# The fourth token form laid with the other three, and one weight unit of each feed-forward group laid at places of its own

## The chip, the core and the metric

The kernel runs on one NeuronCore of a Trainium2 chip. TensorE (PE in the profile) multiplies; before each matmul the stationary operand is loaded into the array by a weight load of its own (PEld). VectorE (DVE), ScalarE (ACT) and GpSimd (POOL) do the element-wise work, SyncE (SP) issues most transfers. The metric is the device time of one execution in microseconds, the median of several runs.

## The reference

A decoder trunk of two layers over 512 tokens of width 1024. Each layer has two feed-forward blocks (inner width 2816), a token mixer (latent attention in layer 0, a sparse attention with compressed, selected and window branches in layer 1) with four memory heads beside it, and three layer norms.

```python
def swiglu(x, w_gu, w_down):
    g, u = jnp.split(x @ w_gu, 2, axis=-1)
    return (jax.nn.silu(g) * u) @ w_down

for layer in range(DEPTH):
    x = layer_norm(DN_ALPHA * x + 0.5 * swiglu(x, ffn_w_gu[layer, 0], ffn_w_down[layer, 0]), ...)
    ...
    x = layer_norm(DN_ALPHA * x + mix, ln_g[layer, 1], ln_b[layer, 1])
    x = layer_norm(DN_ALPHA * x + 0.5 * swiglu(x, ffn_w_gu[layer, 1], ffn_w_down[layer, 1]), ...)
    if layer == N_A_LAYERS - 1:
        shared = nsa_shared_kv(x, nsa_w_kv, cmp_pos, cmp_w1, cmp_b1, cmp_w2)
```

The element type is float32.

## The kernel before

Every float32 operand of a product is held as two parts: `hi`, the value rounded by a cast on ACT, and `lo`, the remainder, taken by DVE (`split`, L199 and L200). A product is then three matmuls, hi by hi, hi by lo and lo by hi. Weights come in units of 128 x 1024 (`wraw`, four places), and each unit is split into `whi` and `wlo`. `prep` does this for the unit that is next in the list of `_unit_order`; `ring` gives it its two places, of seven that are used in turn (three in `wring`, four in `W.extra`).

A feed-forward block (`ffn`) works in five groups of four or five inner slices of 128 (`GROUPS`, 22 slices in all). In a group the slices are computed first, then `by_units` (or `token_major` in the last group) multiplies them by the group's down weights, with 512 columns for a matmul (L411 to L416).

A slice marked `d` is computed by `seven` as seven quarter products in place of eight, in the manner of Strassen: the tokens are 1024 x 512, seen as four quarters, and besides two of the quarters themselves (`quarters`, views of `xhi` and `xlo`) four sums and differences of quarters are used, the token forms `F.t[1]` to `F.t[4]`, made once for each block by `token_forms`. A quarter product (`quarter`, L376, L377 and L380) is twelve matmuls of 256 columns; the weight is the stationary operand, the token quarter streams past it. The weight units of such a slice are `g0` (two quarters on `xhi`/`xlo`), `g1` (form 4, then form 1), `g2` (forms 2 and 3) and `g3` (one quarter, half a unit). A slice marked `s` is computed in the plain way by `feature_major` (L363, L365, L368), 24 matmuls for each half of the tokens and each of its two weights (gate and up). In the first group of a block with `halves` (all blocks but the first of layer 1) the six units of the three `s` slices are held together and go through the first half of the tokens, then through the second.

The order of work on each engine is set by the framework from the program's own order and from when it reckons that operands and places are free; a change of places can thus move instructions.

Where things lie in a partition of SBUF, in bytes from its start, as the program is built: the places of all weight units are at multiples of 256; `xhi`, `xlo` and the forms 1 to 3 are at 192 past a multiple of 256 (`F.xp` begins with an offset of 448 bytes); form 4 is at a multiple of 256, since `open_f` puts an offset of 320 bytes ahead of it. A step of 128 columns is 512 bytes, so an operand keeps this remainder from matmul to matmul. `hhi` and `hlo`, the slices' results and the stationary operand of the down product, are at multiples of 256.

`norm_tile` writes the squares that it needs only as a sum into a scratch tile `junk` (L323, L324), which has a place of its own in the pool `F.sm`.

```python
        for i in (1, 2, 3, 0, 4):
            for e in "hl":
                if i:
                    F.fm.tile([P, 4, 256], F32, tag=f"t{i}{e}", name="place")
            if not i:
                F.fm.tile([P, 80], F32, name="offset")
```

## Time and profile before

| | us |
|---|---|
| median of 3 runs | 1853.71 (1851.89 to 1856.44) |
| the profiled execution | 1853.84 |
| its span, first to last instruction | 1852.1 |
| PE busy | 1830.8 |
| PE weight loads busy | 1650.6 |
| DVE busy | 1463.3 |
| ACT busy | 869.8 |
| POOL busy | 162.6 |

What lies around the span is 1.7 us. TensorE's granted clock is 0.999 over the span, so it ran at the higher of its two levels (2.4 GHz) throughout. Matmuls overlap: the duration of one runs past the start of the next, so what a matmul costs in a stream is read from start to start and not from its duration. A stretch of matmuls without a wait is priced by the start of its first, the start of the first that follows it, and the count between.

### The profile page before, as it was taken

Reading aid. Unit: us, or ns where it says so; the run is one execution under the profiler, and the core shown is the slowest. Engines: PE = TensorE matmul, PEld = TensorE weight load, DVE = VectorE, ACT = ScalarE, POOL = GpSimd, SP = SyncE. Lnnn points to the kernel's source line nnn. Section 1 sums busy time; section 2 is a strip of 40 time slices with the busy share of each in tenths; the row PEclk is TensorE's granted clock in tenths of the full one; section 3 lists DMA queues with packets and bytes.
Section 4 is the critical chain, followed back from the end, with each engine's and each line's share of the span. In section 5 each row is a group of like instructions: output and inputs, shape, how many; then the busy total and the mean of one; then the engine's idle time right before and its main releaser. Section 6 shows DMA issues by size and latency. Waiting matters only on the chain.

```text
span 1852.1 us, 31917 instructions
## 1 busy us (share of the span) xinstructions
PE 1830.8 (99%) x12772; PEld 1650.6 (89%) x12772; DVE 1463.3 (79%) x2365; ACT 869.8 (47%) x1439; POOL 162.6 (9%) x185
## 2 busy tenths in 40 slices
PE   9999999999999999999999999999999999999998
PEld 8899899896789899999999998998956789999997
DVE  8788789758668789788897987987567478887887
ACT  6344345456555335334653433444466444434432
POOL 0000000025500000000100000001255200000000
PEclk9999999999999999999999999999999999999999
DMA  7333335531134233234433323334321323323322
GB/s 243 117 110 118 111 106 154 178 103 34 59 114 149 80 103 126 81 108 143 132 123 109 126 87 108 114 121 158 109 47 28 114 76 130 114 80 115 118 80 77
DMA packets 60277, 203.86 MB, mean 110 GB/s; under 512 B 7008, under 2 KB 7792, under 8 KB 60128
## 3 DMA queue, kind: packets, MB, share of 16 engines
q1 hardware_dynamic: 57424, 194.44, 32.5%
q0 software_dynamic: 2416, 7.11, 1.3%
q8 instruction: 101, 1.65, 0.4%
q14 instruction: 48, 0.39, 0.1%
q10 hardware_dynamic: 288, 0.26, 0.0%
HBM read 188.16 MB, written 7.34 MB: 106 GB/s over the span
## 4 chain that ended last, share of the span: by engine, by line
PE 91%; DVE 4%; ACT 2%; DMA 1%; issue 1%; POOL 1%; POOLq 0%; SPq 0%; DVEq 0%; ACTq 0%
PE bank L376 13%; PE bank L380 13%; PE bank L377 13%; PE bank L411 4%; PE bank L412 4%; PE bank L413 4%; PE bank L415 4%; PE bank L414 4%; PE bank L416 4%; PE bank L365 3%; PE bank L368 3%; PE bank L363 3%; PE tb L671 2%; PE o L699 2%; PE s L1243 1%; PE bank L352 1%
## 5 line engine op out<-in xcount | busy, mean ns | idle before, releaser
L199 ACT CAST whi<-wraw 128x1024 fp32r<-128x1024 f32 (+2 forms) x475 | 460.1, 978 | 550.7 <-PE bank L416 243.9
L200 DVE TENSOR_TENSOR wlo<-wraw,whi 128x1024 fp32r<-128x1024 f32 (+2 forms) x475 | 535.1, 1132 | 131.3 <-ACT whi L199 130.4
L376 PE MATMUL bank<-t,whi 128*128 128x256 f32 x1232 | 298.4, 278 | 0.0
L377 PE MATMUL bank<-t,whi 128*128 128x256 f32 x1232 | 297.9, 278 | 0.0
L377 PEld LDWEIGHTS bank<-t,whi 128*128 128x128 f32 x1232 | 231.9, 188 | 0.0
L376 PEld LDWEIGHTS bank<-t,whi 128*128 128x128 f32 x1232 | 231.9, 188 | 0.0
L376 PE MATMUL bank<-xhi,whi 128*128 128x256 f32 x924 | 222.0, 277 | 0.0
L377 PE MATMUL bank<-xlo,whi 128*128 128x256 f32 x924 | 222.0, 277 | 0.0
L380 PE MATMUL bank<-t,wlo 128*128 128x256 f32 x1232 | 191.8, 278 | 0.0
L376 PEld LDWEIGHTS bank<-xhi,whi 128*128 128x128 f32 x924 | 173.6, 188 | 0.6
L377 PEld LDWEIGHTS bank<-xlo,whi 128*128 128x128 f32 x924 | 173.6, 188 | 0.6
L380 PEld LDWEIGHTS bank<-t,wlo 128*128 128x128 f32 x1232 | 164.2, 189 | 0.0
L315 DVE SCALAR_TENSOR_TENSOR x<-x,bank 128x512 f32<-128x512 f32 x176 | 112.5, 682 | 55.2 <-PE bank L415 53.2
L380 PE MATMUL bank<-xhi,wlo 128*128 128x256 f32 x924 | 143.0, 277 | 0.0
L412 PE MATMUL bank<-whi,hhi 128*128 128x512 f32 x336 | 131.0, 390 | 0.0
L414 PE MATMUL bank<-wlo,hhi 128*128 128x512 f32 x336 | 130.9, 390 | 0.0
L415 PE MATMUL bank<-whi,hlo 128*128 128x512 f32 x336 | 130.8, 389 | 0.0
L411 PE MATMUL bank<-whi,hhi 128*128 128x512 f32 x336 | 130.8, 390 | 0.0
L413 PE MATMUL bank<-wlo,hhi 128*128 128x512 f32 x336 | 130.8, 389 | 0.0
L416 PE MATMUL bank<-whi,hlo 128*128 128x512 f32 x336 | 130.7, 389 | 0.0
L363 PE MATMUL bank<-xhi,whi 128*128 128x256 f32 x520 | 125.0, 281 | 0.0
L365 PE MATMUL bank<-xlo,whi 128*128 128x256 f32 x520 | 124.6, 280 | 0.0
(340 smaller groups left out, 3547.6 us busy)
## 6 DMA issues: line engine op xcount, KB each, us to landing
wraw<-in_gu SPq DMA_DIRECT2D x173, 512.0 KB, 3.3
wraw<-in_dn SPq DMA_DIRECT2D x88, 512.0 KB, 3.8
wraw<-in_wo SPq DMA_DIRECT2D x16, 512.0 KB, 3.4
wraw<-in_wm SPq DMA_DIRECT2D x8, 512.0 KB, 4.1
x_dram<-x SPq DMA_DIRECT2D x8, 512.0 KB, 2.9
x<-x_dram SPq DMA_DIRECT2D x8, 512.0 KB, 4.3
wraw<-in_w SPq DMA_DIRECT2D x8, 512.0 KB, 4.6
wraw<-in_wq SPq DMA_DIRECT2D x6, 512.0 KB, 3.4
```

The costliest lines, as they stand in the source:

```text
L199: nc.scalar.copy(hi, src)
L200: return eng.tensor_tensor(lo, src, hi.bitcast(F32), op=ALU.subtract).ins
L363: nc.tensor.matmul(ps[:, c0:c1], lhsT=hi[:, k * P:(k + 1) * P], rhs=F.xhi[:, k, c0:c1], start=k == 0, stop=False)
L376: nc.tensor.matmul(ps, lhsT=hi[:, ks], rhs=xh[:, k], start=k == 0, stop=False)
L377: nc.tensor.matmul(ps, lhsT=hi[:, ks], rhs=xl[:, k], start=False, stop=False)
L380: nc.tensor.matmul(ps, lhsT=lo[:, ks], rhs=xh[:, k], start=False, stop=k == 3)
L411: nc.tensor.matmul(p0, lhsT=ahi, rhs=hi[:, 0:512], start=first, stop=False)
L412: nc.tensor.matmul(p1, lhsT=ahi, rhs=hi[:, 512:1024], start=first, stop=False)
L413: nc.tensor.matmul(p0, lhsT=ahi, rhs=lo[:, 0:512], start=False, stop=False)
L414: nc.tensor.matmul(p1, lhsT=ahi, rhs=lo[:, 512:1024], start=False, stop=False)
L415: nc.tensor.matmul(p0, lhsT=alo, rhs=hi[:, 0:512], start=False, stop=last)
L416: nc.tensor.matmul(p1, lhsT=alo, rhs=hi[:, 512:1024], start=False, stop=last)
```

## The change

Three things are done to places, and no instruction of the computation is added or removed.

- `open_f` no longer has the offset, so that form 4 lies like the forms 1 to 3, at 192 past a multiple of 256.
- One weight unit of each group gets a pair of places of its own, `aparth` and `apartl`, in the pool of the block, behind an offset of 192 bytes: as built, 192 past a multiple of 256, where all other weights are at multiples of 256. `_unit_order` notes which: in the first block of a layer the unit `g0` of the first `d` slice of each group, in the second block the third unit of the first group (the gate weight of the second `s` slice) and `g0` of the first slice in the other groups. `prep` takes these places for it and does not count it in the ring.
- The scratch of `norm_tile` goes into the place of form 2 (`t2h`).

The pool of the block also places `hhi`, `hlo` and the three `sg` tiles beforehand, in the order in which they lay.

```diff
     def ffn(l, f, s):
         for m0, items in _groups(l, f):
             m = m0
+            apart.add(len(order) + (2 * items.index("d") if f == 0 else 2 * (m0 == 0)))
...
-        hi, lo = ring(scope)
+        hi, lo = [W.apart.tile([P, 1024], F32R, tag="apart" + e, name=n) for e, n in
+                  (("h", "whi"), ("l", "wlo"))] if W.done in apart else ring(scope)
...
-        for i in (1, 2, 3, 0, 4):
+        for i in range(1, 5):
             for e in "hl":
-                if i:
-                    F.fm.tile([P, 4, 256], F32, tag=f"t{i}{e}", name="place")
-            if not i:
-                F.fm.tile([P, 80], F32, name="offset")
+                F.fm.tile([P, 4, 256], F32, tag=f"t{i}{e}", name="place")
...
-        junk = F.sm.tile([P, D], BF16, name="junk", bufs=1)
-        nc.scalar.activation(junk, x, AF.Square, bias=nmu, accum_out=ss)
+        junk = F.fm.tile([P, 2 * D], BF16, tag="t2h", name="junk")
+        nc.scalar.activation(junk[:, :D], x, AF.Square, bias=nmu, accum_out=ss)
...
         hst, hp = right_pool(f"h{l}{f}")
+        for e in "hl":
+            hp.tile([P, 5, T], F32, tag="h" + e, name="place")
+        for e in range(3):
+            hp.tile([P, T], F32, tag="sg", name="place", bufs=3)
+        hp.tile([P, 48], F32, name="offset")
+        for e in "hl":
+            hp.tile([P, 1024], F32, tag="apart" + e, name="place")
+        hp.tile([P, 80], F32, name="rest")
+        W.apart = hp
...
-            hhi = hp.tile([P, 5, T], F32R, tag="hhi", name="hhi")
-            hlo = hp.tile([P, 5, T], F32R, tag="hlo", name="hlo")
+            hhi = hp.tile([P, 5, T], F32R, tag="hh", name="hhi")
+            hlo = hp.tile([P, 5, T], F32R, tag="hl", name="hlo")
```

The instructions move at a few places. On ACT, at the end of each group that is followed by another, the cast of the next group's `g0` comes ahead of the cast of the group's last down unit. In layer 0's second block, first before (`whi_6757` is the last down unit, `whi_6843` is `g0`), then now (`whi_6773` and `whi_6859`):

```order
L199 CAST whi_6729<-wraw_6727 128x1024
L544 COPY us_6626<-bank_6633 128x256
L199 CAST hhi_6102<-gs_6473 128x512
L199 CAST whi_6757<-wraw_6755 128x1024
L199 CAST whi_6843<-wraw_6841 128x1024
```

```order
L204 CAST whi_6745<-wraw_6743 128x1024
L555 COPY us_6642<-bank_6649 128x256
L204 CAST whi_6859<-wraw_6857 128x1024
L204 CAST hhi_6118<-gs_6489 128x512
L204 CAST whi_6773<-wraw_6771 128x1024
```

The last down unit and the cast of `hhi` each stand one cast later, and on DVE the remainders follow in the same way.

On DVE, in the compression of the shared keys and values (`shared_kv`), a gelu is worked out for two windows; `hb_10161` and `u_10162` belong to the first window before, `hb_10177` and `u_10178` now, and PE then transposes `hb`. First before, then now:

```order
L1061 TENSOR_TENSOR u_10162<-u_10162,hb_10161 64x256
L200 TENSOR_TENSOR wlo_10289<-wraw_10286,whi_10288 128x1024
L390 TENSOR_TENSOR wraw_10378<-b_9554,b_9553 128x1024
L1063 TENSOR_SCALAR u_10162<-u_10162 64x256
L1058 TENSOR_TENSOR hb_10244<-bank_10171,b1_9748 64x256
L1064 RECIPROCAL u_10162<-u_10162 64x256
L1059 TENSOR_TENSOR u_10245<-hb_10244 64x256
L1065 TENSOR_TENSOR hb_10161<-hb_10161,u_10162 64x256
```

```order
L1072 TENSOR_TENSOR u_10178<-u_10178,hb_10177 64x256
L1074 TENSOR_SCALAR u_10178<-u_10178 64x256
L1075 RECIPROCAL u_10178<-u_10178 64x256
L1069 TENSOR_TENSOR hb_10260<-bank_10187,b1_9764 64x256
L1076 TENSOR_TENSOR hb_10177<-hb_10177,u_10178 64x256
L1070 TENSOR_TENSOR u_10261<-hb_10260 64x256
L205 TENSOR_TENSOR wlo_10305<-wraw_10302,whi_10304 128x1024
```

A weight remainder (`wlo`) and the first token difference (L390) have left the chain to the first `hb`; the difference now stands behind both windows. On PE the transposes of the first `hb` stand 7 matmuls earlier and those of the second 11 matmuls earlier among the matmuls around them. Ahead of this, the last two units of the second window have changed their order on ACT and DVE.

On DVE, where layer 1's queries are made (`nsa_in`), L203 writes the low part of a pair's queries (`qf`), L735 takes the maxima for the memory heads. First before, then now:

```order
L741 RECIPROCAL ms<-ms 128x4
L200 TENSOR_TENSOR wlo<-wraw,whi 128x1024
L203 SCALAR_TENSOR_TENSOR qf<-bank,qf 128x512
L735 TENSOR_REDUCE mm<-bank 128x2 x2
L741 RECIPROCAL ms<-ms 128x4
```

```order
L752 RECIPROCAL ms<-ms 128x4
L746 TENSOR_REDUCE mm<-bank 128x2
L208 SCALAR_TENSOR_TENSOR qf<-bank,qf 128x512
L746 TENSOR_REDUCE mm<-bank 128x2
L752 RECIPROCAL ms<-ms 128x4
L205 TENSOR_TENSOR wlo<-wraw,whi 128x1024
```

The weight remainder now stands behind the low part of the queries; one maximum has come ahead of it. On POOL the three small loads of layer 0's mixer (`rope` and two `gbc`) now stand among the four steps of the norm (L328) and no longer ahead of them, the two `gbc` between the third and the fourth. On SP one of the transfers of the output weights of layer 0 stands behind five others.

## Rows read from the trace of the kernel before

**Rows 1.** The page: busy time of the engines, and the chain of work that ended last, by engine and by line.

```profile
PE 1830.8 (99%) x12772; PEld 1650.6 (89%) x12772; DVE 1463.3 (79%) x2365; ACT 869.8 (47%) x1439; POOL 162.6 (9%) x185
...
PE 91%; DVE 4%; ACT 2%; DMA 1%; issue 1%; POOL 1%; POOLq 0%; SPq 0%; DVEq 0%; ACTq 0%
PE bank L376 13%; PE bank L380 13%; PE bank L377 13%; PE bank L411 4%; PE bank L412 4%; PE bank L413 4%; PE bank L415 4%; PE bank L414 4%; PE bank L416 4%; PE bank L365 3%; PE bank L368 3%; PE bank L363 3%; PE tb L671 2%; PE o L699 2%; PE s L1243 1%; PE bank L352 1%
```

**Rows 2.** The groups of instructions on PE by line: matmuls of the quarter products, on the forms and on the tokens themselves. L377 and L380 have the same counts.

```profile
L376 PE MATMUL bank<-t,whi 128*128 128x256 f32 x1232 | 298.4, 278 | 0.0
...
L376 PE MATMUL bank<-xhi,whi 128*128 128x256 f32 x924 | 222.0, 277 | 0.0
```

**Rows 3.** The timeline of PE where a group of four `d` slices begins (layer 0, second block, second group). First the last down matmul of the group before, then the first matmul of each quarter product of the first slice (two quarters of `g0`, form 4, form 1, form 2, form 3), then form 4, form 1 and form 2 of the second slice. Columns: start in us, duration, engine, line.

```profile
631.33 0.39 PE L416 MATMUL bank<-whi,hlo 128*128 128x512 f32 x1
631.56 0.28 PE L376 MATMUL bank<-xhi,whi 128*128 128x256 f32 x1
...
632.97 0.28 PE L376 MATMUL bank<-xhi,whi 128*128 128x256 f32 x1
...
634.38 0.28 PE L376 MATMUL bank<-t,whi 128*128 128x256 f32 x1
...
635.82 0.29 PE L376 MATMUL bank<-t,whi 128*128 128x256 f32 x1
...
637.20 0.28 PE L376 MATMUL bank<-t,whi 128*128 128x256 f32 x1
...
638.56 0.28 PE L376 MATMUL bank<-t,whi 128*128 128x256 f32 x1
...
644.00 0.28 PE L376 MATMUL bank<-t,whi 128*128 128x256 f32 x1
...
645.42 0.29 PE L376 MATMUL bank<-t,whi 128*128 128x256 f32 x1
...
646.80 0.28 PE L376 MATMUL bank<-t,whi 128*128 128x256 f32 x1
```

**Rows 4.** The timeline of PE at the first quarter matmul of a group and at the first down matmul behind it: first the first groups of the four blocks, in order (168, 168, 252 and 168 quarter matmuls between), then the end of the group of Rows 3 (336 matmuls), then a group of five slices (420).

```profile
40.38 0.28 PE L376 MATMUL bank<-xhi,whi 128*128 128x256 f32 x1
...
59.58 0.39 PE L411 MATMUL bank<-whi,hhi 128*128 128x512 f32 x1
...
585.03 0.28 PE L376 MATMUL bank<-xhi,whi 128*128 128x256 f32 x1
...
604.34 0.39 PE L411 MATMUL bank<-whi,hhi 128*128 128x512 f32 x1
...
962.96 0.28 PE L376 MATMUL bank<-xhi,whi 128*128 128x256 f32 x1
...
991.88 0.39 PE L411 MATMUL bank<-whi,hhi 128*128 128x512 f32 x1
...
1541.50 0.28 PE L376 MATMUL bank<-xhi,whi 128*128 128x256 f32 x1
...
1560.70 0.39 PE L411 MATMUL bank<-whi,hhi 128*128 128x512 f32 x1
...
670.08 0.39 PE L411 MATMUL bank<-whi,hhi 128*128 128x512 f32 x1
...
691.85 0.28 PE L376 MATMUL bank<-xhi,whi 128*128 128x256 f32 x1
...
739.97 0.39 PE L411 MATMUL bank<-whi,hhi 128*128 128x512 f32 x1
```

**Rows 5.** The timeline of PE in the `s` slices of the second blocks: the first matmul of the second and of the third unit (layer 0, 24 matmuls apart), then in layer 0 and in layer 1 the second matmul behind the transposes of the last token tile, 206 matmuls ahead of the first quarter matmul.

```profile
553.03 0.28 PE L363 MATMUL bank<-xhi,whi 128*128 128x256 f32 x1
...
555.86 0.28 PE L363 MATMUL bank<-xhi,whi 128*128 128x256 f32 x1
...
560.76 0.28 PE L363 MATMUL bank<-xhi,whi 128*128 128x256 f32 x1
...
1518.14 0.28 PE L363 MATMUL bank<-xhi,whi 128*128 128x256 f32 x1
```

**Rows 6.** The waits of PE over the whole span: what waited for what, us in total, times, the longest.

```profile
PE bank L1071 <- DVE hb L1065: 1.1, 1, 1.1
...
PE bank L352 <- DVE qf L203: 0.8, 1, 0.8
...
PE bank L500 <- ACT whi L483: 0.2, 1, 0.2
```

**Rows 7.** The timeline of DVE in `shared_kv` (a weight remainder, the first token difference, the second `hb`) and in `nsa_in` (a weight remainder, the low part of the second pair's queries).

```profile
931.02 1.23 DVE L200 TENSOR_TENSOR wlo<-wraw,whi 128x1024 fp32r<-128x1024 f32 x1 [0.43 <-ACT whi L199]
932.28 1.23 DVE L390 TENSOR_TENSOR wraw<-b 128x1024 f32<-128x1024 f32 x1
...
942.35 0.42 DVE L1065 TENSOR_TENSOR hb<-hb,u 64x256 f32<-64x256 f32 x1
...
1311.68 2.30 DVE L200 TENSOR_TENSOR wlo<-wraw,whi 128x1024 fp32r<-128x1024 f32 x1 [0.76 <-ACT whi L199]
1313.90 0.68 DVE L203 SCALAR_TENSOR_TENSOR qf<-bank,qf 128x512 fp32r<-128x512 f32 x1
```

**Rows 8.** The group of the norm's squares on ACT (last columns: idle time ahead of it and what ended it), and the fourth step of a norm on POOL in the first block.

```profile
L324 ACT ACTIVATE junk<-x,st 128x1024 bf16<-128x1024 f32 x24 | 27.7, 1153 | 38.4 <-DVE st L322 38.2
...
354.83 1.37 POOL L328 TENSOR_TENSOR st<-st,cst 128x1 f32<-128x1 f32 x1 [8.08 <-DVE st L327]
```

More of the change, by code (lines that the diff above doesn't have):

```diff
@@ L54, in _unit_order @@
 def _unit_order():
-    order = []
+    order, apart = [], set()
     def ffn(l, f, s):
@@ L101, in _unit_order @@
     ffn(1, 1, 2)
-    return order
+    return order, apart
 @with_exitstack
@@ L107, in tile_trunk @@
     nc = tc.nc
-    order = _unit_order()
+    order, apart = _unit_order()
     const = ctx.enter_context(tc.tile_pool(name="const", bufs=1))
@@ L123, in tile_trunk @@
         extra = None
+        apart = None
         count = 0
```

## The prediction

> **What bounds the kernel now.** I read the page first [rows 1]: PE is busy for 99% of the span, and the chain of work that ended last runs over PE for 91%. What counts is therefore what PE executes and the few places where it waits. The full list of PE's waits, of which [rows 6] shows three, adds up to 13.6 us and holds none inside a feed-forward group. By lines, the quarter products are the largest part [rows 2]: 3 x (1232 + 924) = 6468 matmuls of one shape. Their own durations (277 and 278 ns) say nothing of a price, since they overlap, so I read the starts.
>
> The starts have more than one spacing [rows 3]. All stretches there are twelve matmuls of 128x256 without a wait. Behind a down product the two quarters of `g0` take 1.41 us each (117.5 ns a matmul). Form 4 takes 1.44 (120 ns), form 1 behind it 1.38, form 2 1.36 (113.3 ns). In the second slice form 4 takes 1.42 and the quarter behind it 1.38. Which operands lie where tells these apart: form 4 and its weights are both at multiples of 256, while forms 1 to 3 and the tokens are at 192 against weights at multiples of 256. So equal remainders cost 6.7 ns a matmul. There is a second thing to see: after the down product PE stays at 117.5 ns although the places of `g0` are the same as later on, and it comes back to 113.3 only behind the first form 4. I call these the slow and the quick step. All of it is at a granted clock of 0.999, so it isn't the clock.
>
> The Trainium skill says otherwise: "TensorE: Matmul & The Clock Gate", section "Step-by-step: what each phase is for", has two independent read ports on PE, so that loading the next weights takes no bandwidth from the running matmul, and "SBUF — State Buffer", section "Who interferes with whom", that PE never waits on anyone. By these the place of a weight or a form could cost nothing, and this part of the sum would be nil; the spacings of [rows 3] don't agree.
>
> **The change part by part.**
>
> *Forms and the weight unit of their own.* What the quarter products lose now is read from [rows 4], at 1.36 us a quarter for twelve matmuls. The group of four slices in the rows takes 670.08 - 631.56 = 38.52, less 28 x 1.36 = 38.08: 0.44. The group of five takes 739.97 - 691.85 = 48.12, less 35 x 1.36 = 47.60: 0.52. The four first groups lose 19.20 - 19.04 = 0.16, 19.31 - 19.04 = 0.27, 28.92 - 28.56 = 0.36 and 19.20 - 19.04 = 0.16. Each block has three more groups of four and one of five: 4 x (3 x 0.44 + 0.52) + 0.95 = 8.31 us.
>
> The offset's removal puts form 4 at 192 against weights at multiples of 256, the relation of form 2, so it runs at the quick step. But form 4 was also what ended the slow step. The unit laid apart takes over this part: it lies at 192 and meets tokens at 192, equal remainders again, for the 24 matmuls of `g0`. Its price is 2 x (1.44 - 1.36) = 0.16, and 0.02 for the quarter behind it: 0.18 in place of 0.44 or 0.52. Eighteen groups have it among their quarter products (the first groups of the two second blocks have it among the `s` slices, and their quarters then lose about nothing): 18 x 0.18 = 3.24. The gain is 8.31 - 3.24 = **5.1 us**, from 4.6 (the quarter behind the unit costs 0.04, or the 0.01 to which rows are given sums against me) to 5.5.
>
> *The third unit of the second blocks' `s` slices.* Unit 2 takes 555.86 - 553.03 = 2.83 us for 24 matmuls, 117.9 ns, so it is at the slow step. In layer 0 this lasts to the first quarter product: 585.03 - 560.76 = 24.27 for 206 matmuls, 117.8 ns, a loss of 206 x 4.5 ns = 0.92. In layer 1 the same stretch takes 23.36, 113.4 ns: quick, since transposes behind which the step may come out either way stand ahead of it [rows 5]. With the units ahead of these transposes (some 80 matmuls at the slow step in each layer, 0.36) and the first quarters (0.11 in layer 0, which is in the sum above) that is 1.64 for both layers. Now the third unit runs once in each half of the tokens. The two units ahead of it stay slow, 0.22, it costs 0.18 twice, and behind the transposes up to 0.49 is lost until it comes again: 0.58 to 1.07 for a layer, 1.16 to 2.14 for both. I take the middle, 1.65: **nothing**, from -0.5 to +0.5.
>
> *Order at the end of each group.* The last down unit and `hhi` are one cast later on ACT, their remainders one split later on DVE. A pass of ACT over a tile of this size takes 1.15 us [rows 8], and the list of PE's waits shows none for a split in any group, so units are ready ahead of their use by more than nothing: I price the exchange at nothing. If the cover were short in a group, PE would wait for at most one remainder, 1.23 as in [rows 7], in each of the 16 groups; that is in the list of what would prove me wrong.
>
> *`nsa_in`.* PE's wait of 0.8 us for `qf` [rows 6] stands behind a weight remainder of 2.30 us that ended at 1313.98, when `qf` ran at once [rows 7]. With the remainder behind `qf` the wait goes: **-0.8**. The remainder is then ahead of the third pair's maxima and `qf`, and its own unit comes up to 1 us later: from -1.0 to +0.3.
>
> *`shared_kv`.* The first `hb` loses a weight remainder and a token difference ahead of it, 1.23 us each [rows 7], so PE's wait of 1.1 [rows 6] goes. What is next is the second `hb`: its two transposes now stand 11 matmuls earlier on PE, about 1.3 us at 117.8 ns, while DVE's chain to it is shorter by only 0.6 to 1.0, as the token difference has left it but the other window's steps stand before it: 0.3 to 0.7 of a wait, where it has none now (0.42 at 942.35 was done in time). And the two units that changed order leave a cast of PE's next weight later, about 0.2, as in the wait for `whi` of [rows 6]. Net -1.1 + 0.5 + 0.2 to the nearest: **-0.2**, allowing for a changed step behind moved transposes from -1.1 to +1.0.
>
> *The rest is priced at nothing.* The square of the norm in form 2's place: its last reader is a matmul of the slices, before the down product ahead of every norm, and ACT idles 38.4 us ahead of these squares, 38.2 of it for DVE [rows 8]; without that cover a square would hold a tile's norm by its own 1.15 us. POOL's two loads between the third and fourth step of a norm: the fourth step waited 8.08 us for DVE [rows 8], longer than two issues take. SP: the transfer of one output weight behind five others is in a stretch in which the list of PE's waits shows none for weights. For these three together I allow 0 to +1.
>
> The sum: -5.1 + 0 - 0.8 - 0.2 = -6.1, against the profiled execution's 1853.84: **1847.7 us**. The median of the runs, 1853.71, is as good as the same, so the forecast is 0.32% below it.
>
> **The rivals.**
>
> *The moves give it back.* The gain on the quarters comes, but the second `hb` is waited for longer (+1.0), the steps behind the transposes come out slow (+0.5) and `nsa_in` shifts its wait (0): 1853.8 - 5.1 + 1.5 = 1850.2. For it: in [rows 5] the same stretch is quick in one layer and slow in the other with nothing different in its places. Against it: three items would have to go the wrong way.
>
> *The slow step isn't ended (slower).* In all that the trace shows, what ended the slow step was a moving operand that came to its weights' remainder (form 4). Now the weights come to the tokens' remainder. If the step doesn't end on that, each group stays slow from the down product on: 18 x 24 = 432 matmuls at 120 ns lose 2.9, the other 6036 at 117.6 lose 4.3 ns each, 25.8: 28.7 where 8.3 is lost now, +20.4 us: 1853.8 - 1.0 + 20.4 = 1873. The point from which it decides is the first matmul of `g1` in each group. Against it: what matters in [rows 3] looks like a relation of both operands, which is the same here whichever moves. A group that stays slow loses 1.3 more than forecast (24 x 6.7 + 312 x 4.3 ns = 1.5 for a group of four), so 5 of them would take the gain and 9 would make the kernel measurably slower.
>
> *Places don't matter.* The spacings would then come from something else that goes with form 4 (its line in the loop, its banks), and the change would only move instructions: 1853.8 - 1.0 = 1852.8. Against it are the equal codes of forms 4 and 2 in [rows 3] with different steps. This is the time by the Trainium skill's rule of the two ports, named above.
>
> *The first `hb` is all gain.* With no new wait behind it and `nsa_in` at its better end, and the quarters at 5.5: 1853.8 - 5.5 - 1.0 - 1.1 = 1846.2, less 0.5 if the `s` slices come out quick: 1845.7.
>
> **How the numbers follow.** The forecast, as the sum with its small ends, 0.56; given back 0.20; all gain 0.12; places don't matter 0.05; slow step not ended 0.07. A measurement of this kernel tells some 0.3%, 5.6 us, from no change: faster is below 1848.15. The forecast's own spread is about 1.5 us each way around 1847.7, so some 0.36 of its 0.56 lies below that, and with the 0.12 of all gain faster has 0.48. Same has the other 0.20 of the forecast, the 0.20 of giving back and the 0.05 of places that don't matter, 0.45. Slower is 0.07. The range goes from 1844.5 (all gain and 1.2 for quick steps at places not counted) to 1852.0 (given back, with 0.8 of the 0 to +1 for the rest and 1.0 for waits at group ends); beyond it are places that don't matter, the slower rival and a few hundredths on the low side.
>
> **What would show it.** In the changed kernel's trace, right: behind a down product both quarters of `g0` at 1.44 us, the next at 1.38, all others of the group at 1.36, form 4 too; a group of four with 0.18 over 38.08; the third unit of the `s` slices at 2.88 for 24; `qf` and the first `hb` gone from PE's waits, the second `hb` there with some tenths; no wait in the group ends. Wrong: `g1` to `g3` at 1.41 (slow step not ended), form 4 still at 1.42 (places don't matter), a wait of PE for a split behind a group's last down unit, or for a norm's `st` longer by the square. The sum would also fail without any of these if the slow step came up in the down products or the mixers, which I took as unchanged.

## The result, and the profile after

The changed kernel takes 1878.8 us (median of 4 runs, 1878.53 to 1881.58) where the kernel before took 1854.1 (4 runs): a ratio of 1.0134, 95% interval 1.0122 to 1.0145. It is 24.7 us slower. I had forecast 1847.7 and 1844.5 to 1852.0. One execution of the run with one extra tile (below), 2020.8 us at a granted clock of 0.848, is left out of its median, since no other execution ran at such a clock.

The page says at once that it is PE's own work and not a wait: 27.1 us more busy time for the same 12772 matmuls, against [rows 1]. The group of matmuls on the forms shows it by its mean: 281 ns where it was 278 [rows 2].

```profile
PE 1857.9 (99%) x12772; PEld 1676.8 (89%) x12772; DVE 1466.4 (78%) x2365; ACT 865.2 (46%) x1439; POOL 162.0 (9%) x185
...
L379 PE MATMUL bank<-t,whi 128*128 128x256 f32 x1232 | 304.2, 281 | 0.0
```

The timeline of PE at the same place as [rows 3], the second group of layer 0's second block: the last down matmul, then the first matmul of each quarter product of the first slice (two quarters of `g0`, then forms 4, 1 and 2), the first down matmul behind the group, and the two ends of the next group.

```profile
641.61 0.39 PE L418 MATMUL bank<-whi,hlo 128*128 128x512 f32 x1
641.83 0.28 PE L378 MATMUL bank<-xhi,whi 128*128 128x256 f32 x1
...
643.27 0.28 PE L378 MATMUL bank<-xhi,whi 128*128 128x256 f32 x1
...
644.70 0.28 PE L378 MATMUL bank<-t,whi 128*128 128x256 f32 x1
...
646.12 0.28 PE L378 MATMUL bank<-t,whi 128*128 128x256 f32 x1
...
647.53 0.28 PE L378 MATMUL bank<-t,whi 128*128 128x256 f32 x1
...
681.45 0.39 PE L413 MATMUL bank<-whi,hhi 128*128 128x512 f32 x1
...
703.25 0.28 PE L378 MATMUL bank<-xhi,whi 128*128 128x256 f32 x1
...
752.76 0.39 PE L413 MATMUL bank<-whi,hhi 128*128 128x512 f32 x1
```

The quarters of `g0` take 1.44 and 1.43, as forecast for equal remainders. But then come 1.42 and 1.41: the slow step (117.5 ns a matmul) goes on behind the unit laid apart, and it does so to the end of the group. The group takes 681.45 - 641.83 = 39.62, 1.54 over 38.08, where it was 0.44 [rows 4]; the group of five 49.51, 1.91 over 47.60, where it was 0.52. Read in this way at all twenty groups, the quarter products lose 29.5 us where they lost 8.3: **21.2 of the 24.7 us are here.**

In the `s` slices of the second blocks one sees the same thing from the other side. The timeline of PE in layer 1, second half of the tokens: the first matmul of each of four units, 24 matmuls apart; the second here (1552.46) is the one laid apart.

```profile
1549.74 0.28 PE L365 MATMUL bank<-xhi,whi 128*128 128x256 f32 x1
...
1552.46 0.28 PE L365 MATMUL bank<-xhi,whi 128*128 128x256 f32 x1
...
1555.34 0.28 PE L365 MATMUL bank<-xhi,whi 128*128 128x256 f32 x1
...
1558.16 0.28 PE L365 MATMUL bank<-xhi,whi 128*128 128x256 f32 x1
```

2.72, then 2.88 for the unit laid apart, then 2.82 (117.5 ns a matmul). The unit ahead of it ran at the quick step, 113.3 ns. The unit laid apart not only fails to end the slow step, it starts it.

The profiled execution of the changed kernel is 1881.58 us, 2.8 above the median. The windows of its first microseconds show one reason (columns: stretch, us, busy time of PE, PEld, DVE, ACT and POOL, granted clock, DMA share, GB/s); first after, then before.

```profile
8.00:14.00 6.00, 5.60 (x26) 5.60 (x27) 4.59 (x9) 5.16 (x9) 0.00 (x0) 0.50 1.05 372
```

```profile
8.00:14.00 6.00, 5.93 (x52) 5.93 (x53) 5.26 (x10) 5.16 (x9) 0.00 (x0) 1.00 1.04 367
```

It began at the lower level of the clock (0.50, 1.2 GHz), the one before at the higher, and ran half as many matmuls in these 6 us. So the first group of quarters starts at 44.50 and not at 40.38 [rows 4]. I take this for chance and not for the change, though no kernel was traced twice: of the thirteen traces here eight show the lower level somewhere between 6 and 14 us and five don't, and the changed kernel with a shift (below) is among the five. I leave these 4.1 us out by counting from the first quarter matmul on.

The waits of PE, those that answer to [rows 6] (what waited for what, us in total, times, the longest):

```profile
PE bank L353 <- ACT hT L204: 1.5, 1, 1.5
...
PE bank L354 <- DVE wlo L205: 0.7, 1, 0.7
...
PE bank L354 <- DVE qf L208: 0.4, 1, 0.4
```

The wait for the first `hb` is gone, and another of 1.5 has come two steps further on, for the cast of `hT` (what PE's transposes of `hb` become). The wait for `qf` is halved. The one for a weight remainder is new; it stands in `shared_kv` too, 8 us ahead of the one for `hT` (944.26 below, at a matmul on `zh`, the input of the compression). All waits of PE in the list add up to 13.6 us; the list of before adds up to 12.9, and not to the 13.6 that I wrote there.

The wait for `hT` costs more than its 1.5 us. A window of the changed kernel behind its end, columns as above, then PE's timeline at the two new waits and behind them:

```profile
953.00:956.00 3.00, 3.00 (x17) 3.00 (x16) 1.15 (x2) 0.06 (x1) 0.00 (x0) 0.50 0.73 202
```

```profile
944.26 0.33 PE L354 MATMUL bank<-wlo,zh 128*64 128x256 f32 x1 [0.69 <-DVE wlo L205]
...
952.33 0.30 PE L353 MATMUL bank<-hT,whi 128*128 128x64 f32 x1 [1.47 <-ACT hT L204]
...
953.86 0.41 PE L354 MATMUL bank<-wlo,xhi 128*128 128x256 f32 x1
954.07 0.41 PE L355 MATMUL bank<-whi,xlo 128*128 128x256 f32 x1
```

PE stood for 1.47 us, and soon after, the granted clock is 0.50 for 3 us, the lower of the two levels: matmuls of 256 columns start 213 ns apart, where 117 is their step at the higher level. Some 15 of them in these 3 us lose 15 x 0.096 = 1.4 us. Such a fall doesn't always come: in the kernel before the clock stayed at its higher level behind PE's waits of 1.1 (`hb`) and 1.9 us, and so it did in the changed kernel behind another wait, of 1.6 us.

### The profile page after: what moved, and what is told of

It reads as the page before. It is cut to its first block, busy times and chain, and to the rows that moved or that the text cites. A ratio compares the mean times of both kernels' runs of the same rounds, so it can differ in the third digit from the quotient of the medians.

```text
span 1879.8 us, 31903 instructions
## 1 busy us (share of the span) xinstructions
PE 1857.9 (99%) x12772; PEld 1676.8 (89%) x12772; DVE 1466.4 (78%) x2365; ACT 865.2 (46%) x1439; POOL 162.0 (9%) x185
## 3 DMA queue, kind: packets, MB, share of 16 engines
q8 instruction: 101, 1.65, 0.4%
## 4 chain that ended last, share of the span: by engine, by line
PE 92%; DVE 3%; ACT 1%; DMA 1%; POOL 1%; issue 1%; SPq 0%; POOLq 0%; DVEq 0%; ACTq 0%
PE bank L379 14%; PE bank L382 14%; PE bank L378 14%; PE bank L413 4%; PE bank L415 4%; PE bank L414 4%; PE bank L417 4%; PE bank L416 4%; PE bank L418 4%; PE bank L370 3%; PE bank L367 3%; PE bank L365 3%; PE tb L682 2%; PE o L710 2%; PE bank L355 2%; PE bank L354 2%
## 5 line engine op out<-in xcount | busy, mean ns | idle before, releaser
L379 PE MATMUL bank<-t,whi 128*128 128x256 f32 x1232 | 304.2, 281 | 0.0
L378 PE MATMUL bank<-t,whi 128*128 128x256 f32 x1232 | 304.2, 281 | 0.0
L379 PE MATMUL bank<-xlo,whi 128*128 128x256 f32 x924 | 228.6, 281 | 0.0
L378 PE MATMUL bank<-xhi,whi 128*128 128x256 f32 x924 | 228.6, 281 | 0.0
L382 PE MATMUL bank<-xhi,wlo 128*128 128x256 f32 x924 | 146.8, 281 | 0.0
L330 POOL TENSOR_TENSOR st<-st,cst 128x1 f32<-128x1 f32 x24 | 16.8, 701 | 1502.6 <-DVE st L329 1502.5
L365 PE MATMUL bank<-xhi,whi 128*128 128x256 f32 x520 | 125.7, 282 | 0.0
```

Source lines behind the costliest of these rows:

```text
L365: nc.tensor.matmul(ps[:, c0:c1], lhsT=hi[:, k * P:(k + 1) * P], rhs=F.xhi[:, k, c0:c1], start=k == 0, stop=False)
L378: nc.tensor.matmul(ps, lhsT=hi[:, ks], rhs=xh[:, k], start=k == 0, stop=False)
L379: nc.tensor.matmul(ps, lhsT=hi[:, ks], rhs=xl[:, k], start=False, stop=False)
L382: nc.tensor.matmul(ps, lhsT=lo[:, ks], rhs=xh[:, k], start=False, stop=k == 3)
```

## The experiments

**Which part does it: the units laid apart, or form 4?** First the changed kernel without units laid apart.

```diff
-        hi, lo = [W.apart.tile([P, 1024], F32R, tag="apart" + e, name=n) for e, n in
-                  (("h", "whi"), ("l", "wlo"))] if W.done in apart else ring(scope)
+        hi, lo = ring(scope)
```

> The changed kernel with all weight units back in the ring, so that no weight meets tokens or a form at an equal remainder anywhere. Theory (an equal remainder ends the slow step only if the way out of it is a change of the moving operand's place, and the units laid apart never ended it): each group of four stays at the slow step, 336 x 4.4 ns = 1.5 us over 38.08 as in the changed kernel, and the time is 1876 to 1879, a little below the changed kernel's 1878.8, since 18 x 24 matmuls at 120 ns are gone. Rival (the units laid apart themselves put PE into the slow step, and without them it is quick): 0 to 0.1 us over 38.08 in a group and 1846 to 1849 us.

1874.66 us, ratio 1.011 (1.0095 to 1.0125). The timeline at the first quarter matmul and the first down matmul of the group of four as above:

```profile
637.79 0.28 PE L377 MATMUL bank<-xhi,whi 128*128 128x256 f32 x1
...
677.37 0.39 PE L412 MATMUL bank<-whi,hhi 128*128 128x512 f32 x1
```

39.58, 1.50 over 38.08. So the group is slow without any equal remainder in it, and the units laid apart add only 0.04 to it: they are not what makes it slow. The first group of layer 0's second block came out quick in this run (19.04 us for 168), as its `s` slices were quick, and the time is a little below the range that I gave.

Then the changed kernel with form 4 back at a multiple of 256 and the units laid apart kept.

```diff
-        for i in range(1, 5):
+        for i in (1, 2, 3, 0, 4):
             for e in "hl":
-                F.fm.tile([P, 4, 256], F32, tag=f"t{i}{e}", name="place")
+                if i:
+                    F.fm.tile([P, 4, 256], F32, tag=f"t{i}{e}", name="place")
+            if not i:
+                F.fm.tile([P, 16], F32, name="offset")
...
-        hp.tile([P, 80], F32, name="rest")
+        hp.tile([P, 16], F32, name="rest")
```

> The changed kernel with form 4 back at a multiple of 256 (an offset of 64 bytes ahead of it does that; to make room the rest behind the units laid apart is 64 bytes in place of 320). Theory (the loss is the missing form 4 alone): g0 at 1.44 us a quarter, form 4 at 1.44, then 1.36: a group of four loses 0.49 over 38.08 in place of 0.44 before, and the time is 1854 to 1856. Rival (a unit laid apart leaves a slow step that form 4 doesn't end either): 1.5 over 38.08 and 1877 to 1880.

1858.15 us, ratio 1.0022 (1.0011 to 1.0033), in the same group:

```profile
633.11 0.28 PE L381 MATMUL bank<-xhi,whi 128*128 128x256 f32 x1
...
671.67 0.39 PE L416 MATMUL bank<-whi,hhi 128*128 128x512 f32 x1
```

38.56, 0.48 over 38.08: form 4 ends the slow step here too, right behind a unit that doesn't. The time is 3.5 us above the kernel before on the same chip and above the range that I gave. Of this 9.3 - 8.3 = 1.0 is in the quarter products. Of the rest the waits that came with the moved instructions are a part: they are those of the changed kernel (`hT` 1.6, `wlo` 0.6, `qf` 0.4), and in this profiled execution the clock falls behind the wait for `hT` as it does there. Its window over the end of that wait (939.11) and behind it:

```profile
938.00:941.00 3.00, 1.89 (x9) 1.89 (x10) 2.76 (x5) 1.48 (x4) 0.00 (x0) 0.68 0.37 126
```


**Why does form 4 end it and the unit laid apart not?** Both meet an equal remainder for a stretch. Two things differ. Form 4 met its weights at 0, the unit laid apart meets the tokens at 192. And behind form 4 it is the moving operand whose place changes, behind the unit laid apart the stationary one. Laying the left side of SBUF 64 bytes further, in the kernel before and in the changed one, tells these apart.

```diff
+    shift = ctx.enter_context(tc.tile_pool(name="shift", bufs=1))
+    shift.tile([P, 16], F32, name="shift")
     wring = ctx.enter_context(tc.tile_pool(name="wring", bufs=NRING))
```

> The kernel before with everything on the left side of SBUF from the weight ring on laid 64 bytes further: weights and form 4 at 64 past a multiple of 256, tokens and forms 1 to 3 at 0; all differences as before, hhi and hlo unchanged. Theory A (what decides is which operand's place changes at the way out of equal remainders: the moving one's here): as before, 0.44 over 38.08 in a group of four, 1852 to 1857. Theory B (what decides is the place itself: equal at 0 ends quick, equal elsewhere ends slow): 1.5 to 1.7 over 38.08 and 1876 to 1882.

> The changed kernel with the same 64 bytes: weights of the ring at 64, tokens and all forms at 0, and the units laid apart at 0, so that equal remainders are met at 0, as form 4 met them before. Theory A (the way out is by the stationary operand's place): slow as the changed kernel, 1.5 over 38.08 in a group of four, 1876 to 1880. Theory B (equal at 0 ends quick): 0.18 over 38.08 and 1846 to 1850.

(The changed kernel also loses the 192 bytes ahead of the units laid apart, so that these lie at 0.) 1859.58 us, ratio 1.0026 (1.0016 to 1.0035), and 1891.36, 1.0202 (1.0185 to 1.0219). The timeline of the kernel before with the shift: first down matmul of the group ahead, the first matmuls of `g0`'s two quarters, of forms 4, 1 and 2, and the first down matmul behind the group.

```profile
606.20 0.39 PE L413 MATMUL bank<-whi,hhi 128*128 128x512 f32 x1
...
633.67 0.28 PE L378 MATMUL bank<-xhi,whi 128*128 128x256 f32 x1
...
635.05 0.28 PE L378 MATMUL bank<-xhi,whi 128*128 128x256 f32 x1
...
636.41 0.28 PE L378 MATMUL bank<-t,whi 128*128 128x256 f32 x1
...
637.83 0.29 PE L378 MATMUL bank<-t,whi 128*128 128x256 f32 x1
...
639.21 0.28 PE L378 MATMUL bank<-t,whi 128*128 128x256 f32 x1
...
672.09 0.39 PE L413 MATMUL bank<-whi,hhi 128*128 128x512 f32 x1
```

And of the changed kernel with the shift, the ends of the group:

```profile
645.08 0.28 PE L380 MATMUL bank<-xhi,whi 128*128 128x256 f32 x1
...
684.70 0.40 PE L415 MATMUL bank<-whi,hhi 128*128 128x512 f32 x1
```

This kernel also waits for `hT`; its wait, and the window behind it (granted clock 1.00):

```profile
957.63 0.30 PE L355 MATMUL bank<-hT,whi 128*128 128x64 f32 x1 [1.40 <-ACT hT L206]
```

```profile
958.00:961.00 3.00, 3.00 (x28) 3.00 (x28) 1.96 (x5) 0.60 (x3) 0.00 (x0) 1.00 0.70 216
```

Form 4 at 64 costs 1.42 and leaves PE quick, 38.42 in all; units laid apart at 0 leave it slow, 39.62 as without the shift. And among the `s` slices of layer 0's second block the unit laid apart at 0 again starts the slow step: 113.3 ns a matmul ahead of it, 117.8 behind. So the place itself isn't it: theory B falls, and theory A's forecast for the group comes true in both, though both times lie above the ranges that I gave. What I had not expected is that the group comes out of the down product quick here (1.38 and 1.36 for `g0`). In the kernel before the down product has equal remainders, the moving operand leaves them for 192, and PE is slow behind it; here its operands are 64 apart. So an equal remainder that the moving operand leaves can also be followed by the slow step, and theory A as I put it holds for the quarter matmuls only. The shift also set `hhi` and the down weights 64 bytes apart, and the down product pays for it: 633.67 - 606.20 = 27.47 for 120 matmuls where it was 631.56 - 604.34 = 27.22 [rows 3, 4], 0.25 each time. That is most of why the time is 5 us above the kernel before though its quarters lose less (6.8 us). In the changed kernel with the shift the down product comes in slow as well, which is where its further 12 us are.

**Does it matter that form 4 and the next form share a weight unit?** The kernel before with the two lines exchanged.

```diff
-                quarter(p45[:, c0], w, 512, *F.t[4])
                 quarter(p45[:, c1], w, 0, *F.t[1])
+                quarter(p45[:, c0], w, 512, *F.t[4])
```

> The kernel before with form 1 ahead of form 4 in each slice: the way out of the equal remainder is then at the change from unit g1 to unit g2, and no longer inside one unit. Theory (what counts is that the moving operand's place changes): quick behind form 4 all the same; 12 matmuls more at the slow step in a group, 0.49 over 38.08, 1854 to 1856 us. Rival (what counts is that the weight unit stays the same on the way out): slow through the group, 1.5, 1876 to 1879.

1856.42 us, ratio 1.0007 (0.9997 to 1.0016). The first matmuls of `g0`, of forms 1, 4, 2, and of the down product:

```profile
633.25 0.28 PE L376 MATMUL bank<-xhi,whi 128*128 128x256 f32 x1
...
636.07 0.28 PE L376 MATMUL bank<-t,whi 128*128 128x256 f32 x1
...
637.49 0.28 PE L376 MATMUL bank<-t,whi 128*128 128x256 f32 x1
...
638.92 0.29 PE L376 MATMUL bank<-t,whi 128*128 128x256 f32 x1
...
671.82 0.39 PE L411 MATMUL bank<-whi,hhi 128*128 128x512 f32 x1
```

Form 1 is now one more slow quarter (1.42), form 4 ends it at the change of the unit, 38.57 in all, 0.49 over 38.08 as expected. So it doesn't.

**How much of an equal remainder does it take?** All units in the ring as in the first run, and only the low part of form 4 at a multiple of 256.

```diff
         for i in range(1, 5):
             for e in "hl":
+                if (i, e) == (4, "l"):
+                    F.fm.tile([P, 16], F32, name="offset")
                 F.fm.tile([P, 4, 256], F32, tag=f"t{i}{e}", name="place")
```

> All weight units in the ring, and of form 4 only the low part at a multiple of 256 (64 bytes of offset between its two parts); its high part at 192. Of the twelve matmuls of form 4 four then meet an equal remainder, one at a time between others, and the moving operand leaves it each time. Theory (one such return by the moving operand ends the slow step): 0.11 for g0, then 0.03 to 0.06 for each form 4, so 0.25 to 0.35 over 38.08 in a group of four where the kernel before has 0.44, and 1850 to 1853 us. Rival (it takes a run of equal matmuls, or both parts): 1.5 over 38.08 and 1874 to 1877.

1850.37 us, ratio 0.998 (0.997 to 0.999), 0.28 or 0.29 over 38.08 in a group of four: it ends the slow step, for half the price of form 4. Then one matmul of the first slice only, with an extra tile.

```diff
+        F.fm.tile([P, 16], F32, name="offset")
+        F.fm.tile([P, 256], F32, tag="t5", name="place")
...
+            if i == 4:
+                F.t5 = F.fm.tile([P, 256], F32R, tag="t5", name="t")
+                nc.vector.tensor_tensor(F.t5, u[:, 3], F.t[4][0][:, 3], op=ALU.subtract)
...
-            nc.tensor.matmul(ps, lhsT=hi[:, ks], rhs=xl[:, k], start=False, stop=False)
+            nc.tensor.matmul(ps, lhsT=hi[:, ks], rhs=x3 if x3 is not None and k == 3 else xl[:, k], start=False, stop=False)
...
-                quarter(p45[:, c0], w, 512, *F.t[4])
+                quarter(p45[:, c0], w, 512, *F.t[4], F.t5 if j == first else None)
```

> All weight units in the ring, all forms at 192, and one extra tile of 128x256 at a multiple of 256 that holds the last quarter of form 4's low part a second time; only the first d slice of each group uses it, so that one matmul in a group meets an equal remainder. Theory (one return of the moving operand from an equal remainder ends the slow step): g0 slow (0.11), form 4 slow up to that matmul (0.05), then quick to the end of the group: 0.16 to 0.2 over 38.08 in a group of four, 3.5 for all groups where the kernel before loses 8.3, and 1848 to 1851 us. Rival (one is too short; several are needed): 1.5 over 38.08 and 1873 to 1877 us.

1849.09 us (7 executions), ratio 0.9966 (0.9955 to 0.9977). The timeline of the ends of two groups: the group of four, and the first group of layer 1's first block, the latter with the matmul of the `s` slices that stands 144 ahead of it (944.09).

```profile
631.00 0.28 PE L379 MATMUL bank<-xhi,whi 128*128 128x256 f32 x1
...
669.25 0.39 PE L417 MATMUL bank<-whi,hhi 128*128 128x512 f32 x1
...
944.09 0.28 PE L366 MATMUL bank<-xhi,whi 128*128 128x256 f32 x1
...
961.05 0.28 PE L379 MATMUL bank<-xhi,whi 128*128 128x256 f32 x1
...
990.73 0.40 PE L417 MATMUL bank<-whi,hhi 128*128 128x512 f32 x1
```

38.25, 0.17 over 38.08, so one matmul is enough here; but 29.68, 1.12 over 28.56, in the other: there the slow step came out of the `s` slices ((961.05 - 944.09) / 144 = 117.8 ns), and one matmul didn't end it. The first groups of the other three blocks say nothing, since PE came into them quick (`g0` at 1.36 a quarter); the one matmul ended the slow step in the 16 groups behind a down product. In the next run `g1` (form 4, then form 1) comes ahead of `g0` in the first slice of each group, in `_unit_order`, in the loads of `combined` and in `seven`; and in the run behind it the tile holds two quarters.

```diff
-                    order.extend((f"g{i}", (l, f, m), 1024, s) for i in range(4))
+                    head = m == m0 + items.index("d")
+                    order.extend((n, (l, f, m), 1024, s) for n in (("G1", "G0", "g2", "g3") if head else
+                                                                  ("g0", "g1", "g2", "g3")))
...
-        F.fm.tile([P, 256], F32, tag="t5", name="place")
+        F.fm.tile([P, 2, 256], F32, tag="t5", name="place")
```

> As the run with one extra tile, and in the first d slice of each group the unit g1 (form 4, then form 1) comes ahead of g0, so that g0's 24 matmuls are behind the way out. Theory: 0.05 to 0.08 over 38.08 in a group of four, some 1.5 for all groups, 1846 to 1849 us, unless the two loads that the unit now in front waits for show up as a wait of PE at the start of a group. Rival (one matmul is too short): 1.5 over 38.08 and 1873 to 1877 us.

> As the run with g1 ahead of g0, but the extra tile holds the last two quarters of form 4's low part, so that two matmuls of the first form 4 in a group meet an equal remainder, with one at 192 between them. In the run with one such matmul the slow step went on through the first group of layer 1's first block (1.12 over 28.56), where it came out of the s slices, and ended in all 19 others. Theory (a return of the moving operand can miss, and another one behind it meets PE at another moment): that group ends quick too, 0.05 to 0.1 over 28.56, 0.07 in the others, some 1.2 for all groups, and the time is about 1 us below the run with one. Rival (a slow step that comes out of the s slices isn't ended by so few): 1.1 again in that group.

1848.9 us, ratio 0.9966 (0.9954 to 0.9978), and 1847.93, 0.9966 (0.9952 to 0.998). With one matmul the group of layer 1 came in slow again and stayed slow (29.68). The two groups with the pair, the second again with the matmul of the `s` slices 144 ahead of it (945.41):

```profile
631.92 0.28 PE L386 MATMUL bank<-t,whi 128*128 128x256 f32 x1
...
670.04 0.39 PE L424 MATMUL bank<-whi,hhi 128*128 128x512 f32 x1
...
945.41 0.28 PE L373 MATMUL bank<-xhi,whi 128*128 128x256 f32 x1
...
961.73 0.28 PE L386 MATMUL bank<-t,whi 128*128 128x256 f32 x1
...
990.32 0.39 PE L424 MATMUL bank<-whi,hhi 128*128 128x512 f32 x1
```

38.12 and 28.59: 0.04 and 0.03 over the quick step. But the second of them proves nothing for the pair: this time the `s` slices ahead of it ran at (961.73 - 945.41) / 144 = 113.3 ns, so there was no slow step to end. Whether two matmuls end one that comes out of the `s` slices stays open, and the expectation's 19 groups were 16. Longer pieces did end such a step: four matmuls (form 4's low part, in layer 0's second block) and the whole of form 4 (the kernel before, in the same place). All twenty groups together lose 0.8 us where the kernel before loses 8.3. This is the fastest version that I ran; of the 7.5 us some 6.4 show in the time, and the intervals of the last three runs don't part them.

**What counts as equal?** All units in the ring, the tokens and all forms at another place.

```diff
-        F.xp.tile([P, 112], F32, name="offset")
+        F.xp.tile([P, 96], F32, name="offset")
```

> All weight units in the ring, tokens and all forms at 128 past a multiple of 256 in place of 192. If the remainder that counts is that of 128, every quarter matmul meets an equal one: 6468 x 6.7 ns = 43 us where the kernel before loses 8.3, the s slices and the mixers' matmuls on tokens too, and the time is 1890 to 1900 us. If it is that of 256, this is a place like 192: 0 to 1.5 us over 38.08 in a group of four and 1846 to 1877 us.

> All weight units in the ring, tokens and all forms at 160 past a multiple of 256. Theory (only an equal remainder matters, any other difference has the quick and the slow step): slow behind each down product, 1.5 over 38.08 in a group of four, 1874 to 1877 us as with 192. Rival (the slow step belongs to a difference of 64, and at another there is none): 0 to 0.1 over 38.08, 1846 to 1849 us. Third (a difference of 32 is half an equal one): 113.3 to 120 ns in every matmul with no change along a group, 1865 to 1890 us.

(For the second of these the tile has 104 elements.) 1892.86 us, ratio 1.0206 (1.0185 to 1.0227), and 1883.01, 1.0154 (1.0139 to 1.0169). The group of four at 128 past a multiple of 256, then at 160:

```profile
643.53 0.28 PE L377 MATMUL bank<-xhi,whi 128*128 128x256 f32 x1
...
683.84 0.39 PE L412 MATMUL bank<-whi,hhi 128*128 128x512 f32 x1
```

```profile
640.28 0.28 PE L377 MATMUL bank<-xhi,whi 128*128 128x256 f32 x1
...
680.15 0.39 PE L412 MATMUL bank<-whi,hhi 128*128 128x512 f32 x1
```

40.31 / 336 = 120.0 ns: at a distance of 128 the matmuls pay the price of equal remainders, so it is the remainder of 128 that counts. That is so in 17 of the 20 groups; the three first groups that start behind both halves of the `s` slices run at 118.6 ns, as those slices do (19.93 us for 168, from 596.36 in layer 0's second block), so this distance has two steps as well. 39.87 / 336 = 118.7 ns at a distance of 32: dearer than the slow step at 64, and the same in all groups. A step of 113.3 ns was only seen at the distance of 64.

## Why the prediction was wrong

**The step that failed** is in the first part, "The unit laid apart takes over this part: it lies at 192 and meets tokens at 192, equal remainders again". The price that I gave it was right (1.44 a quarter), the state behind it wrong. An equal remainder is not enough to end the slow step: with the weights as the ones whose place changes at the way out of it, PE is slow behind it, whether it was slow ahead of it (the groups) or quick (1555.34 above). In the quarter products what ended it was an equal remainder that the moving operand leaves while the weights keep theirs. The runs hold this up: form 4 put back ends it behind a unit laid apart, the shift by 64 bytes changes neither case, the exchange of two forms neither, and a few matmuls of form 4 suffice. But the side is not the whole condition. The down product has equal remainders too (`hhi` and its weights at multiples of 256), the moving operand leaves them for 192, and all 16 groups behind it start slow (1.41 [rows 3]). And a unit laid apart differs from form 4 also in its 24 matmuls and in its pool, which no run parts from the side. That the loss is the missing end of the slow step is shown; why one equal stretch ends it and another doesn't stays open beyond this, and so does why PE keeps such a state.

**The rival was there.** "The slow step isn't ended" named the mechanism and the point from which it decides (the first matmul of `g1`), at 1873 us and a chance of 0.07. I argued against it that what matters "looks like a relation of both operands". In the trace of before all ends of the slow step inside the groups were on one side (the moving operand changed), so nothing in it spoke for the other side. And it held a case against a mere relation: the down product has the equal one, and PE is slow behind it [rows 3]. The two should have had like chances at least. The rival's own sum was 6 us short: the quarters lost 21.2 more and not 20.4, and the small terms below went up where I had them go down.

**Form 4 at the quick step** was right in its relation (its matmuls now step like those of form 2) but without worth, since all of them are slow.

**The third unit of the `s` slices**: forecast -0.5 to +0.5. By the matmuls' steps layer 0 lost 0.1 more and layer 1 0.5 more, 0.6 in all, through the unit laid apart that turned a quick stretch slow. Two more stretches of `s` slices changed their step with no change in their places: the first block's lost 0.9 more (216 matmuls, quick before, slow after; quick again in the run with form 4 put back), layer 1's first block 0.4 less. Such stretches start behind transposes or a wait and come out either way.

**The down product** I took as unchanged. It starts 0.03 dearer behind each group, 21.80 for 96 matmuls where it took 691.85 - 670.08 = 21.77 [rows 4], 0.5 in all.

**`nsa_in`**: forecast -0.8, measured -0.5: the wait for `qf` shrank from 0.8 to 0.4 and didn't go; that lies within the bounds. **`shared_kv`**: forecast -0.2 and at worst +1.0, measured +2.5: the wait of 1.1 went as said; 1.5 came, not for the second `hb` but for the cast of `hT` behind the transposes; 0.7 came for a weight remainder, where the sum had 0.2 for the units that changed their order; and the clock took another 1.4. The waits come from the moved instructions: the two other kernels with units laid apart have the one for `hT` as well (1.6 and 1.4), and the first run, with all units in the ring, has none, but 1.6 for `hb`. The fall of the clock is not a fixed price of them: it came behind `hT` in two of the three kernels and not in the third (958.00 above). A price of the clock stood nowhere in my sum.

**Priced at nothing and rightly so**: the exchange at the group ends, the squares in form 2's place, POOL's loads and SP's transfer. No wait of PE in the list of after belongs to them.

The sum, from the first quarter matmul to the end: 1835.3 against 1811.7, +23.6. Of this 21.2 are the quarters, 0.6 and -0.4 the `s` slices of the other blocks, 0.5 the down products, 1.4 the clock, and 0.2 the sum of all waits behind that point (10.2 against 10.0): 23.5. With 0.9 for the first block's `s` slices, which lie ahead of it, that is the 24.7 of the medians within 0.3. The rule of the Trainium skill that I weighed ("TensorE: Matmul & The Clock Gate", section "Step-by-step: what each phase is for"), that loading weights takes no bandwidth from the running matmul, is not borne out: by it the four runs with all units in the ring and tokens or forms at other places (1874.66, 1850.37, 1892.86 and 1883.01) would have had one time, but for moved instructions.

## What to carry to other kernels

Where a profile shows one instruction at two or three spacings in a stream without waits, look for what the last change of spacing followed, and list on which side (moving or stationary, first or second) all its cases lie: a rule that was only ever seen from one side is a guess on the other. Before a costly piece is removed, ask what state it leaves for the work behind it: form 4 cost 0.08 us a time and saved 1.0 a group. If such a piece is needed, make it small, here one or two matmuls in a group in place of 48, rather than moving the job to the other operand.

## What was unexpected of the hardware

- Matmuls of 128x256 with a weight load each stood 113.3 or 117.8 ns apart where the remainders of 128 bytes of weights and moving operand were 64 apart, 118.7 where they were 32 apart, and 118.3 to 120.0 where they were equal, at one clock.
- At a distance of 64 both steps last for hundreds of matmuls with the same places (336 at 117.8, 39.58 us, in the run with all units in the ring; 336 at 113.5, 38.12, in the last one).
- Of the 19 waits of PE of 1.4 to 1.9 us behind the opening in the thirteen traces, six were followed by some 3 us at a granted clock of 0.50, among them the wait for `hT` in two kernels (1.47 and 1.65 us); 13 were not, among them one of 1.9 us in the kernel before.
- One matmul at an equal remainder, left by the moving operand, ended the slow step in all 16 groups behind a down product (two runs), and in neither run the one that came out of the `s` slices of layer 1's first block.
- In the kernel before PE came into the down product quick and out of it slow in all 16 groups that another group follows; with the operands of the down product 64 apart and not equal (the kernel before with the shift) PE came out of it quick.
